# Opening, norms and the products behind them in a hybrid layer: order of the sums, engine of u's second form, banks of the transposes, order of the matmuls

## The chip, the cores and the metric

The kernel runs on one core of a Trainium2 chip. The core has TensorE (PE in the profile; its weight load is PEld), VectorE (DVE), ScalarE (ACT), GpSimd (POOL) and SyncE (SP), which issues most transfers. The metric is the device time of one execution in microseconds; the kernel before has a median of 1338.59 us over 3 runs (1337.43 to 1339.16).

## The reference

One layer over 512 tokens of 1024 channels, all in f32, with nine modulation vectors (three shifts sh, three scales sc, three gates g) made from one conditioning vector c:

```
mod = silu(c) @ w_ada + b_ada                    # 9 vectors of 1024
u = rms_norm(x, g1n) * (1 + sc1) + sh1
x = x + 0.5 * g1 * swiglu(u, ffn1_w_in, ffn1_w_out)      # hidden width 2816
u = rms_norm(x, mix_norm_g) * (1 + sc2) + sh2
z = u @ w_mix + b_mix        # q, k, v, o and gates of an mLSTM; q, k, v and gate of 16 attention heads; 2 merge gates
merged = sigmoid(g_a) * (mlstm branch @ w_branch_a) + sigmoid(g_b) * (attention branch @ w_branch_b)
x = x + g2 * (merged @ w_out)
u = rms_norm(x, ffn2_norm_g) * (1 + sc3) + sh3
x = x + 0.5 * g3 * swiglu(u, ffn2_w_in, ffn2_w_out)
```

`swiglu(u, w_in, w_out)` splits `u @ w_in` into a and b and returns `(silu(a) * b) @ w_out`. The mLSTM's q and k pass a causal convolution of width 4 first.

## The kernel before, in words

**Split products.** Every f32 product is made of three TensorE products of rounded parts: a number is split into a high part (rounded to fp32r) and a low part (the number minus its high part). `mm3` (L108 to L114) issues high × high (L112), high × low of the moving operand (L113) and low × high (L114) into one PSUM bank. `split` (L85 to L96) splits a block of weights that a transfer has put into a raw tile: ScalarE writes the high part wh (L93), VectorE the low part wl (L95). There are three raw tiles and four slots each for wh and wl, so a fifth block's split waits until the last matmul of the first block has read its slot. `w_stat` loads and splits one block of 128 output columns for all 8 channels of 128 (8 × 128 × 128 weights, a 128x1024 tile).

**u.** The normed and modulated activations are kept transposed, as eight channels k of 128 rows by 512 tokens, in two parts uh[k] and ul[k]. `xnorm` makes x times the reciprocal root of its mean square (tiles xn, L236 and L237; the sums of squares are L203, the twelve small steps of the root L129 to L139). `norm_turn` (L261) transposes xn of 256 tokens on TensorE: 16 transposes (L266) into four PSUM banks, channel k in bank k % 4, half k // 4 of the bank. Then `u_from` (L241) per channel: ScalarE reads the bank and writes uh = scale · t + shift (L245), VectorE reads the same and writes the same in full precision as uf (L249), and ul = uf − uh is made by VectorE for even k and by GpSimd for odd k (L250). `norm_half` is the norm and its transposes for one half of the tokens.

**Banks.** There are eight PSUM banks: four called g (`gbank`) for products and four called t (`tbank`), both taken in rotation. A fifth g bank is the first one again, once its reader is through.

**Who sets the order.** All code outside the opening is written in program order and laid out by the framework's planner: it builds each engine's list beforehand, from its own costs, taking the earliest in the program among what it believes ready. Each engine then works through its list strictly in order, waiting on semaphores. The opening, `start` (L680 to L901), is ordered by hand instead: each of its instructions is chained behind the one before on its engine (`queued`, L675).

**The opening.** Shift and scale of the first norm are sums over w_ada: for each block k of 128 columns, VectorE accumulates eight products of a 128x256 tile with a column of silu(c) (`product`, L777 to L786, line L784 in the trace; `ada_dve` is a run of them), TensorE adds up the 128 rows (`total`, L793), ScalarE makes the two columns m (`mods`, L797 and L798), then both uh and uf of channel k (`uh`, L803 and L804), and VectorE ul (`ul`, L806). Meanwhile TensorE multiplies the channels that are ready by the first 3 + 3 column blocks of ffn1 (`mms`, L824: 18 matmuls a channel into 6 banks), whose weights are split at L810 (`wh`) and L814 (`wl`). One round of the loop, k = 3 to 7, is: 12 matmuls of channel k − 1 with the transposes of channel k between them, `total(k)`, the first product of block k + 1 (on ScalarE), the split of the weights of k + 1, products 1 to 3 of block k + 1, `mods(k)`, `uh(k)`, `ul(k)`, products 4 to 7, and the last 6 matmuls of channel k − 1. The six banks are a0, b0, a1, b1, a2, b2 of three ffn blocks; in a channel all six get high × high first, then the product with wl, then the one with ul, except in the last channel, which goes bank by bank.

**Behind the mix norm.** ffn1's output runs in `pair_out`. Four hooks in it (`chans`) make the u's of the first 256 tokens, channels i and i + 4 at a time. Then four blocks of w_mix are multiplied with the first 256 tokens (L1318 ff.), the second half is transposed and made into u, and the same four blocks are multiplied with tokens 256 to 511, one block's bank after another (L1340). Behind that come the convolutions (`qk_conv`, L944 ff., which read those banks) and the gates' product (`gates`, L904 ff., a 128-wide stationary block of 96 columns whose weights are split at L93 from the tile rawg).

**Behind norm 3.** w_out runs over the second half of the columns, with the transposes and u's of the first 256 tokens begun before its last token block (`last`, L1455 ff.); the last three of its weight blocks stay in their slots until that token block has used them. Then `norm_half(1)`, and FFN2, which begins with `first_pair` (L568): the blocks a0, b0, a1, b1 with tokens 0 to 255, one bank after another, then the same with tokens 256 to 511; when a block's two banks are complete, `hidden` (L355) reads them: SiLU on ScalarE (L363), the product on VectorE (L364).

Of the kernel before, what the change touches and what calls it, by code (L numbers as in the profile page):

```python
# [14 lines left out]
AF = mybir.ActivationFunctionType  # L15
# [5 lines left out]
P = 128  # L21
# [27 lines left out]
class Layer:  # L49
# [190 lines left out]

    def u_from(self, ps, k, c0, w, G, sh, pool, start=False):  # L241

        nc = self.nc
        uf = self.tmp(pool, "uf")
        nc.scalar.activation(self.uh[k][:, c0:c0 + w], ps, AF.Identity, scale=G, bias=sh)  # L245
        if start:
            self.last_uf = nc.scalar.activation(uf[:, :w], ps, AF.Identity, scale=G, bias=sh)
        else:
            nc.vector.tensor_scalar(uf[:, :w], ps, G, sh, op0=MUL, op1=ADD)  # L249
        self.last_ul = (nc.gpsimd if not start and k % 2 else nc.vector).tensor_tensor(  # L250
            self.ul[k][:, c0:c0 + w], uf[:, :w], self.uh[k][:, c0:c0 + w], op=SUB)

# [8 lines left out]
    def norm_turn(self, hf, xn, G, sh, b, ks=range(NK)):  # L261

        nc = self.nc
        for k in range(NK):
            for i in range(2):
                nc.tensor.transpose(b[k % 4][:, k // 4 * 256 + i * P:k // 4 * 256 + (i + 1) * P],  # L266
                                    xn[i][k // 4][:, k % 4 * P:(k % 4 + 1) * P], self.ident)
        u = lambda k: self.u_from(b[k % 4][:, k // 4 * 256:(k // 4 + 1) * 256], k, hf * 256, 256, G[:, k:k + 1], sh[:, k:k + 1], self.tp)
        for k in ks:
            u(k)  # L270
        return u

    def gemm_stat(self, ps, w, c0, c1, ks=range(NK)):
        wh, wl = w
        for k in ks:
            self.mm3(ps[:wh.shape[2], c0:c1], wh[:, k, :], wl[:, k, :],
                     self.uh[k][:, c0:c1], self.ul[k][:, c0:c1], k == 0, k == NK - 1)


    def ada_row(self, v, accs, bank):  # L280
# [288 lines left out]
    def first_pair(self, w_in):  # L569

        js = (0, 1)
        wa = [self.w_stat(w_in, j * P) for j in js]
        wb = [self.w_stat(w_in, FF + j * P) for j in js]
        pp = [(self.gbank(), self.gbank()) for _ in js]
        for c0 in (0, 256):
            for i, j in enumerate(js):
                self.gemm_stat(pp[i][0], wa[i], c0, c0 + 256)
                self.gemm_stat(pp[i][1], wb[i], c0, c0 + 256)
                if c0:
                    self.hidden(pp[i][0], pp[i][1], j)  # L580

# [102 lines left out]
    def start(self, st, tp):  # L684
# [128 lines left out]
        def wl(k, eng=None):  # L813
# [3 lines left out]
            else:  # L817
                dve(f(V))
        order = [(b, p) for p in range(3) for b in range(2 * NJ0)]
        def mms(k, n0, n1):  # L820
            h, l = wsp[k]
            for bnk, p in (sorted(order) if k == NK - 1 else order)[n0:n1]:
                c = slice(bnk // 2 * P, (bnk // 2 + 1) * P)
# [46 lines left out]
        wh(3)  # L870
        ada_dve(3, range(0, 3))
        ul(2)
        wl(3)
        ada_dve(3, range(3, 8))
        mms(1, 12, 18)
        for k in range(3, NK):
# [5 lines left out]
            if more:  # L882
                product(k + 1, 0, AC)
                if early:
                    wh(k + 1)
                    wl(k + 1)
                ada_dve(k + 1, range(1, 4))
            mods(k)
            uh(k)
            ul(k)  # L890
            if more:
                if not early:
                    wh(k + 1)
                    wl(k + 1)
                ada_dve(k + 1, range(4, 8))
            mms(k - 1, 12, 18)
# [393 lines left out]
    def run(self):  # L1290
# [8 lines left out]
        with tc.tile_pool(name="f1t", bufs=1) as tp:  # L1299
# [4 lines left out]
            with tc.tile_pool(name="f1h", bufs=1) as fp:  # L1304
# [12 lines left out]
                def chans(i):  # L1317
                    for k in (i, i + 4):  # L1318
                        n2["u"](k)
# [18 lines left out]
        self.qk = [None] * 8  # L1338
        with tc.tile_pool(name="gates", bufs=1) as mp:
            for m in range(4):  # L1340
                self.gemm_stat(pp[m], ws[m], 256, 512)
            for m in range(4):
# [149 lines left out]
```

## Time and profile before

| | |
|---|---|
| median of 3 runs | 1338.59 us |
| the profiled execution | 1337.66 us, span 1335.9 us |
| TensorE busy | 1315.4 us, 6468 matmuls and transposes |
| VectorE / ScalarE / GpSimd busy | 938.9 / 620.7 / 162.3 us |
| read and written | 199.97 MB and 29.95 MB |
| TensorE clock | full speed in every slice |

All times are microseconds from the start of the span unless marked ns. The profiled execution's time is 1.76 us longer than the span that its trace shows. "Waits" are idle time of an engine just before an instruction, put down to the instruction that released it. A name such as `ul<-uf,uh` gives the output and the inputs of an instruction.

### The profile page before, as it was taken

The page shows a single profiled execution, that of the slowest core. Times are in us where ns is not written, and L with a number is a line of the kernel's source. Part 1 is how long each engine was busy: PE and PEld are TensorE (multiplying, and loading weights), DVE is VectorE, ACT ScalarE, POOL GpSimd, SP SyncE. Part 2 cuts the span into 40 slices and gives each one's busy share as a digit, 9 for nine tenths or more (in the row PEclk, how much of TensorE's full clock was granted, in tenths as well). Part 3 has the DMA queues.
Part 4 walks back from the last instruction along what each step waited for, and adds up shares of the span by engine and source line. Part 5 has one row for each costly group of instructions (what it writes and reads, how often), then busy time and mean ns, then how long its engine had stood idle before and what let it go on. Part 6 is the DMA issues. An engine that isn't in the chain of part 4 may idle for free.

```text
span 1335.9 us, 17955 instructions
## 1 busy us (share of the span) xinstructions
PE 1315.4 (98%) x6468; PEld 1101.6 (82%) x6468; DVE 938.9 (70%) x1706; ACT 620.7 (46%) x1056; POOL 162.3 (12%) x216
## 2 busy tenths in 40 slices
PE   7899999999999999999999999999999999999998
PEld 6688888888888888888888878888788888888887
DVE  6777687778678876876585876766676665655655
ACT  5543433326557745556565675432354333433442
POOL 2000000001020100312041311002120000000000
PEclk9999999999999999999999999999999999999999
DMA  9786576776662434444343442787527554444474
GB/s 288 226 274 204 183 235 201 258 235 225 226 161 80 135 111 124 132 116 123 79 143 87 113 128 71 231 250 229 164 88 269 189 181 159 148 151 145 154 260 142
DMA packets 228621, 231.11 MB, mean 173 GB/s; under 512 B 12274, under 2 KB 183954, under 8 KB 228532
## 3 DMA queue, kind: packets, MB, share of 16 engines
q1 hardware_dynamic: 217428, 186.34, 46.5%
q0 software_dynamic: 11040, 43.61, 8.9%
q8 instruction: 51, 0.84, 0.3%
q14 instruction: 38, 0.31, 0.1%
q10 hardware_dynamic: 64, 0.02, 0.0%
HBM read 199.97 MB, written 29.95 MB: 172 GB/s over the span
## 4 chain that ended last, share of the span: by engine, by line
PE 88%; DVE 5%; DMA 3%; ACT 2%; issue 1%; SPq 0%; POOL 0%; DVEq 0%; ACTq 0%; POOLq 0%
PE g L114 21%; PE g L113 21%; PE g L112 21%; PE t L467 2%; PE t L469 2%; PE t L468 2%; PE t L1226 2%; DMA raw<-in_ffn_w_in_dram 2%; PE t L442 1%; PE t L440 1%; PE t L441 1%; PE t L1196 1%; PE t L112 1%; PE t L113 1%; PE t L114 1%
## 5 line engine op out<-in xcount | busy, mean ns | idle before, releaser
L93 ACT ACTIVATE wh<-raw 128x1024 fp32r<-128x1024 f32 x218 | 226.6, 1043 | 385.8 <-PE g L113 99.1
L113 PE MATMUL g<-ul,wh 128*128 128x512 f32 (+2 forms) x984 | 369.9, 376 | 1.1 <-DVE ul L250 0.8
L112 PE MATMUL g<-uh,wh 128*128 128x512 f32 (+2 forms) x984 | 370.1, 377 | 0.7 <-ACT sl L363 0.7
L114 PE MATMUL g<-uh,wl 128*128 128x512 f32 (+2 forms) x984 | 369.6, 376 | 0.2 <-DVE wl L95 0.2
L95 DVE TENSOR_TENSOR wl<-raw,wh 128x1024 fp32r<-128x1024 f32 x218 | 267.2, 1229 | 143.0 <-ACT wh L93 135.9
L113 PEld LDWEIGHTS g<-ul,wh 128*128 128x128 f32 (+1 forms) x984 | 184.9, 188 | 34.7 <-DVE ul L250 1.0
L112 PEld LDWEIGHTS g<-uh,wh 128*128 128x128 f32 (+1 forms) x984 | 184.6, 188 | 34.5 <-ACT sl L363 1.1
L114 PEld LDWEIGHTS g<-uh,wl 128*128 128x128 f32 (+1 forms) x984 | 184.8, 188 | 34.0 <-DVE wl L95 0.4
L112 PE MATMUL g<-wh,uh 128*128 128x512 f32 (+1 forms) x320 | 111.9, 350 | 0.0
L114 PE MATMUL g<-wh,ul 128*128 128x512 f32 (+1 forms) x320 | 111.1, 347 | 0.0
L113 PE MATMUL g<-wl,uh 128*128 128x512 f32 (+1 forms) x320 | 111.0, 347 | 0.0
L291 DVE SCALAR_TENSOR_TENSOR acc<-raw,ccol,acc 128x1024 f32<-128x1024 f32 (+1 forms) x63 | 65.8, 1060 | 41.9 <-DMA raw<-in_w_ada_dram 41.8
L112 PEld LDWEIGHTS g<-wh,uh 128*128 128x128 f32 x320 | 60.5, 189 | 7.8 <-DVE tk L1080 0.5
L114 PEld LDWEIGHTS g<-wh,ul 128*128 128x128 f32 x320 | 60.5, 189 | 7.8
L113 PEld LDWEIGHTS g<-wl,uh 128*128 128x128 f32 x320 | 60.5, 189 | 7.4
L364 DVE TENSOR_TENSOR hp<-g,sl 128x512 f32<-128x512 f32 x43 | 29.5, 688 | 50.2 <-PE g L114 49.4
L430 POOL DMA_DIRECT2D S_d<-rw x22 | 12.2, 555 | 322.7 <-DVE rw L425 303.9
L112 PE MATMUL g<-yl,wh 128*128 128x512 f32 x128 | 50.3, 393 | 0.0
L113 PE MATMUL g<-yl,wh 128*128 128x512 f32 x128 | 50.3, 393 | 0.0
L114 PE MATMUL g<-yl,wl 128*128 128x512 f32 x128 | 50.3, 393 | 0.0
L417 ACT ACTIVATE wh<-rw 128x1024 fp32r<-128x1024 f32 x22 | 23.3, 1057 | 49.5 <-issue 35.7
L1178 ACT ACTIVATE S<-S,mn 128x128 f32<-128x128 f32 (+1 forms) x64 | 35.6, 557 | 20.1 <-DVE mn L1170 12.6
(337 smaller groups left out, 2304.2 us busy)
## 6 DMA issues: line engine op xcount, KB each, us to landing
raw<-in_ffn_w_in_dram SPq DMA_DIRECT2D x82, 512.0 KB, 3.9
raw<-in_w_ada_dram SPq DMA_DIRECT2D x56, 512.0 KB, 4.1
raw<-in_w_mix_dram SPq DMA_DIRECT2D x48, 512.0 KB, 4.1
rw<-in_ffn_w_out_dram POOLq DMA_DIRECT2D x20, 1024.0 KB, 7.1
S_d<-rw POOLq DMA_DIRECT2D x22, 768.0 KB, 4.0
raw<-S_d SPq DMA_DIRECT2D x30, 512.0 KB, 3.8
raw<-in_w_mix_dram SPq DMA_DIRECT2D x32, 256.0 KB, 3.0
ar<-in_w_ada_dram SPq DMA_DIRECT2D x14, 512.0 KB, 7.8
```

The costliest lines, as they stand in the source:

```text
L93: self.last_hi = nc.scalar.activation(hi, src, AF.Copy)
L95: self.last_lo = self.last_wl = (eng or nc.vector).tensor_tensor(lo, src, hi, op=SUB)
L112: mm(ps, lh, rh, start=start, stop=False)
L113: mm(ps, lh, rl, start=False, stop=False)
L114: self.last_mm = mm(ps, ll, rh, start=False, stop=stop)
L291: nc.vector.scalar_tensor_tensor(a, r[:, cut(i)], self.ccol[:, k:k + 1], a, op0=MUL, op1=ADD)
L364: nc.vector.tensor_tensor(h, ps_b[:, c0:c1], s[:, :c1 - c0], op=MUL)
L467: mm(ps[t], a[0], wh[:, k, :], start=first and c + k == 0, stop=False, skip_group_check=True)
L468: mm(ps[t], a[0], wl[:, k, :], start=False, stop=False, skip_group_check=True)
L469: mm(ps[t], a[1], wh[:, k, :], start=False, stop=end, skip_group_check=True)
L1178: nc.scalar.activation(S[:, ws], S[:, ws], AF.Exp, scale=-1.0, bias=m, accum_out=sm[:, qb:qb + 1])
L1226: nc.tensor.matmul(po[:, q0:], vt[pr][:, kb, i % 2, :], Px[:, o:o + T - q0], start=n == 1, stop=n == 8)
```

## The change

Four places are edited.

- `u_from`: ScalarE writes both uh and uf, and VectorE alone makes ul, for every channel.
- `norm_turn`: channel k is put into bank k // 2, half k % 2, so that two neighbouring channels share a bank; the hooks in ffn1's output make channels 2i and 2i + 1 at a time.
- A new function `gemms` multiplies channel by channel over four banks. `first_pair` uses it for all channels of the first 256 tokens, and for channels 0 to 5 of the others; channels 6 and 7 then follow per block (its two banks), with SiLU and product behind each block. The products of the mix norm's second half do the same: channels 0 to 5 over the four banks, then 6 and 7 bank by bank.
- The opening: one product of the sums more stands ahead of each `ul` (products 1 to 4 before and 5 to 7 after it, in place of 1 to 3 and 4 to 7; for block 3, products 0 to 3, `ul(2)`, products 4 to 7, then the split's low part). The last channel's 18 matmuls begin with the eight that need no ul in banks 0 to 3, then the four with ul, then banks 4 and 5.

```diff
-    def u_from(self, ps, k, c0, w, G, sh, pool, start=False):
+    def u_from(self, ps, k, c0, w, G, sh, pool):
...
         nc.scalar.activation(self.uh[k][:, c0:c0 + w], ps, AF.Identity, scale=G, bias=sh)
-        if start:
-            self.last_uf = nc.scalar.activation(uf[:, :w], ps, AF.Identity, scale=G, bias=sh)
-        else:
-            nc.vector.tensor_scalar(uf[:, :w], ps, G, sh, op0=MUL, op1=ADD)
-        self.last_ul = (nc.gpsimd if not start and k % 2 else nc.vector).tensor_tensor(
-            self.ul[k][:, c0:c0 + w], uf[:, :w], self.uh[k][:, c0:c0 + w], op=SUB)
+        nc.scalar.activation(uf[:, :w], ps, AF.Identity, scale=G, bias=sh)
+        self.last_ul = nc.vector.tensor_tensor(self.ul[k][:, c0:c0 + w], uf[:, :w], self.uh[k][:, c0:c0 + w], op=SUB)
...
-                nc.tensor.transpose(b[k % 4][:, k // 4 * 256 + i * P:k // 4 * 256 + (i + 1) * P],
+                nc.tensor.transpose(b[k // 2][:, k % 2 * 256 + i * P:k % 2 * 256 + (i + 1) * P],
...
+    def gemms(self, ps, ws, c0, c1, ks=range(NK)):
+        for k in ks:
+            for p, w in zip(ps, ws):
+                self.gemm_stat(p, w, c0, c1, (k,))
...
         for c0 in (0, 256):
-            for i, j in enumerate(js):
-                self.gemm_stat(pp[i][0], wa[i], c0, c0 + 256)
-                self.gemm_stat(pp[i][1], wb[i], c0, c0 + 256)
-                if c0:
-                    self.hidden(pp[i][0], pp[i][1], j)
+            banks, ws = [p for q in pp for p in q], [w for q in zip(wa, wb) for w in q]
+            self.gemms(banks, ws, c0, c0 + 256, range(6 if c0 else NK))
+            for i, j in enumerate(js if c0 else ()):
+                self.gemms(pp[i], (wa[i], wb[i]), 256, 512, (6, 7))
+                self.hidden(pp[i][0], pp[i][1], j)
...
+        close = sorted(order[:12], key=lambda t: t[0] > 1)
+        close = close[:4] + [(2, 0), (2, 1), (3, 0), (3, 1), (0, 2), (1, 2), (2, 2), (3, 2)] + [(b, p) for b in (4, 5) for p in range(3)]
...
-            for bnk, p in (sorted(order) if k == NK - 1 else order)[n0:n1]:
+            for bnk, p in (close if k == NK - 1 else order)[n0:n1]:
...
-        ada_dve(3, range(0, 3))
+        ada_dve(3, range(0, 4))
         ul(2)
+        ada_dve(3, range(4, 8))
         wl(3)
-        ada_dve(3, range(3, 8))
...
-                ada_dve(k + 1, range(1, 4))
+                ada_dve(k + 1, range(1, 5))
...
-                ada_dve(k + 1, range(4, 8))
+                ada_dve(k + 1, range(5, 8))
...
-                    for k in (i, i + 4):
+                    for k in (2 * i, 2 * i + 1):
...
+            self.gemms(pp, ws, 256, 512, range(6))
             for m in range(4):
-                self.gemm_stat(pp[m], ws[m], 256, 512)
+                self.gemm_stat(pp[m], ws[m], 256, 512, (6, 7))
```

More of the change, by code (lines that the diff above doesn't have):

```diff
@@ L265, in norm_turn @@
             for i in range(2):
-                nc.tensor.transpose(b[k % 4][:, k // 4 * 256 + i * P:k // 4 * 256 + (i + 1) * P],
+                nc.tensor.transpose(b[k // 2][:, k % 2 * 256 + i * P:k % 2 * 256 + (i + 1) * P],
                                     xn[i][k // 4][:, k % 4 * P:(k % 4 + 1) * P], self.ident)
-        u = lambda k: self.u_from(b[k % 4][:, k // 4 * 256:(k // 4 + 1) * 256], k, hf * 256, 256, G[:, k:k + 1], sh[:, k:k + 1], self.tp)
+        u = lambda k: self.u_from(b[k // 2][:, k % 2 * 256:(k % 2 + 1) * 256], k, hf * 256, 256, G[:, k:k + 1], sh[:, k:k + 1], self.tp)
         for k in ks:
```

## Prediction

> **What bounds the kernel now.** I read the profile's page first (its busy times and the chain that ended last), then the waits of TensorE, then windows and timelines around the places that the diff touches.
>
> ```profile
> PE 1315.4 (98%) x6468; PEld 1101.6 (82%) x6468; DVE 938.9 (70%) x1706; ACT 620.7 (46%) x1056; POOL 162.3 (12%) x216
> ...
> PE 88%; DVE 5%; DMA 3%; ACT 2%; issue 1%; SPq 0%; POOL 0%; DVEq 0%; ACTq 0%; POOLq 0%
> ```
>
> TensorE (PE) is busy for 1315.4 of the span of 1335.9 us, so it idles for 20.5 us in all, and the chain runs through it for 88%. The edits add and remove no matmul. They can shorten the time only where PE waits, and lengthen it wherever they let PE wait anew. The waits of PE that stand at lines the edits touch:
>
> ```profile
> PE t L793 <- DVE ac L784: 2.6, 3, 1.4
> PE g L824 <- ACT uh L803: 1.6, 2, 1.2
> ...
> PE g L113 <- DVE ul L250: 0.8, 1, 0.8
> PE g L112 <- ACT sl L363: 0.7, 1, 0.7
> PE g L824 <- DVE ul L806: 0.7, 1, 0.7
> ...
> PE g L113 <- POOL ul L250: 0.3, 1, 0.3
> ```
>
> (columns: total us, times, longest.) Without L112's, which no edit aims at, they sum to 6.0 us, 0.45% of the span: that is the ceiling of what can be won. L793, L803 and L806 lie in the opening, L250 behind the mix norm. None of the five lies behind norm 3, which the edits touch too.
>
> **Part A, the opening** (one more product of the modulation's sum ahead of each ul; the last channel's matmuls in another order).
>
> ```profile
> 12.00:47.40 35.40, 31.91 (x180) 25.43 (x179) 27.31 (x62) 17.91 (x33) 0.00 (x0) 1.00 1.15 307
> ...
> 47.40 0.85 ACT L810 ACTIVATE wh<-raw 128x768 fp32r<-128x768 f32 x1 [2.77 <-DMA raw<-in_ffn_w_in_dram]
> ```
>
> (Windows: bounds, length, busy time of PE, PE's weight load, VectorE, ScalarE and GpSimd, then clock, DMA share, GB/s. Timelines: start, duration, engine, line, operation, and in brackets the idle time before it and what ended that.) Until 47.40 us the transfers are the limit: their share is 1.15 at 307 GB/s, and ScalarE stands 2.77 us until the weights of channel 6 land at 47.40. ScalarE's list is in order, so the uh of channel 5 comes behind that split whatever VectorE did before. Whatever the longer runs of products save ahead of that moment (the L793 waits; the longest is 1.4) is therefore given back at 47.40. I cost the first re-ordering at 0 (were the landing not the limit, it would be −1.4 and more; 307 GB/s excludes that). After it:
>
> ```profile
> 56.06 0.69 DVE L806 TENSOR_TENSOR ul<-uf,uh 128x512 fp32r<-128x512 f32 x1 [0.52 <-ACT uf L804]
> 56.67 2.04 DVE L784 SCALAR_TENSOR_TENSOR ac<-ar,ccol,ac 128x256 f32<-128x256 f32 x4
> ...
> 58.76 0.71 PE L793 MATMUL t<-one,ac 128*128 128x128 f32 x4
> ```
>
> A fourth product (2.04/4 = 0.51) fills VectorE's hole of 0.52 ahead of ul, so the sum is ready at 58.2 instead of 58.7. But PE comes to it at 58.76 without having waited: its 18 matmuls and the transposes fill the time. So 0 again, at most 0.3.
>
> ```profile
> 61.23 0.39 PE L824 MATMUL g<-uh,wl 128*128 128x512 f32 x1
> ...
> 62.28 0.50 PE L824 MATMUL g<-ul,wh 128*128 128x512 f32 x1 [0.66 <-DVE ul L806]
> ...
> 66.00:257.00 191.00, 191.00 (x845) 157.73 (x843) 143.89 (x188) 69.88 (x90) 10.76 (x18) 1.00 0.70 224
> ```
>
> In the kernel before, the last channel goes bank by bank, and its third matmul waits for ul (61.23 + 0.24 to 62.28: some 0.8 with the restart). The new order issues eight matmuls that need no ul first, 8 × 0.23 = 1.9 us, so ul is there. What follows is 191 us in which PE never idles, so the gain stays. Two banks close later than they did (after the ninth and tenth matmul, not the third and sixth); the next block's hiding place is those 191 us. **A = −0.8**, bounds −1.1 (0.8 + 0.3) and +0.1 (SiLU of block 0 four matmuls, 0.9 us, later and uncovered).
>
> **Part B, behind the mix norm** (ScalarE makes uh and uf, VectorE alone ul, channels 2i and 2i+1 share a bank, products by channel over four banks). The first half of the tokens:
>
> ```profile
> 362.00:384.08 22.08, 22.08 (x103) 18.00 (x102) 17.70 (x26) 11.85 (x20) 5.79 (x4) 1.00 0.55 166
> ...
> L249 DVE TENSOR_SCALAR uf<-t,G,sh 128x256 f32<-128x256 f32 x16 | 8.0, 537 | 3.0 <-ACT uh L245 3.0
> ...
> L245 ACT ACTIVATE uh<-t,sh,G 128x256 fp32r<-128x256 f32 x16 | 7.5, 572 | 0.6 <-PE t L266 0.6
> ```
>
> (The last two are groups from norm 3, with two halves of eight: busy us, mean ns, idle time before.) Here PE is full with ffn1's output. Per half, VectorE loses 8 uf (4.0 us) and gets four more ul; ScalarE gains 8 operations at 7.5/16 = 0.47, 3.8 us on top of 11.85 in 22.08. Both fit: 0; with that cover gone the last channel's uf, 0.5, would come late. The second half is where PE waits:
>
> ```profile
> 395.58 1.91 PE L266 MATMUL t<-ident,xn 128*128 128x128 f32 x16
> ...
> 396.88 3.77 ACT L245 ACTIVATE uh<-t,sh,G 128x256 fp32r<-128x256 f32 x8 [2.28 <-PE t L266]
> ...
> 397.49 0.74 PE L112 MATMUL g<-uh,wh 128*128 128x256 f32 x4
> ...
> 399.06 0.39 PE L113 MATMUL g<-ul,wh 128*128 128x256 f32 x1 [0.83 <-DVE ul L250]
> ...
> 399.98 0.39 PE L113 MATMUL g<-ul,wh 128*128 128x256 f32 x1 [0.30 <-POOL ul L250]
> ...
> 410.74 0.39 PE L112 MATMUL g<-uh,wh 128*96 128x512 f32 x1
> ```
>
> 96 matmuls stand between 397.49 and the gates' first at 410.74: 13.25 us for 96 × 0.121 = 11.6, so 1.6 are lost. In the new order bank 0 is full after four transposes instead of ten, so uh starts 6 × 0.12 = 0.7 earlier, at 396.2; then 2 × 0.47 = 0.94 a channel on ScalarE against 12 × 0.121 = 1.45 on PE. The ul of channel 0 is out at 397.8, when PE has done the four matmuls that it can without it. No stall is left: −1.6. Against it, the slot and bank of the first weights, which are used through to the last channels:
>
> ```profile
> 404.58 0.84 ACT L93 ACTIVATE wh<-rawg 128x768 fp32r<-128x768 f32 x1 [3.94 <-PE g L113]
> ...
> 405.46 0.96 DVE L95 TENSOR_TENSOR wl<-rawg,wh 128x768 fp32r<-128x768 f32 x1 [1.85 <-ACT wh L93]
> ```
>
> The split of the gates' weights waits for the slot of the first block, freed at 404.6. Now that is 78 matmuls after 397.4, 406.8; wh and wl are through at 406.8 + 0.84 + 0.96 = 408.6, with PE due at 409.1. It holds by 0.5. If ScalarE or VectorE takes a conv operation first, one turn for a 1024-wide weight (1.06 + 1.22, rows below) lies bare: −1.6 + 2.3 = +0.7. **B = −1.6**, bounds −1.7 and +1.2 (that, and the 0.5 of the first half). I take the low end, because the planner put this split ahead of the conv before.
>
> **Part C, behind norm 3.** Nothing waits there, but the weights stand in ScalarE's list behind the u's:
>
> ```profile
> 978.99 3.74 ACT L245 ACTIVATE uh<-t,sh,G 128x256 fp32r<-128x256 f32 x8
> 982.59 2.99 ACT L93 ACTIVATE wh<-raw 128x1024 fp32r<-128x1024 f32 x3
> 987.05 0.63 ACT L203 ACTIVATE rs<-x 128x512 f32<-128x512 f32 x1 [1.48 <-DVE x L670]
> ...
> 985.14 1.22 DVE L95 TENSOR_TENSOR wl<-raw,wh 128x1024 fp32r<-128x1024 f32 x1
> ...
> 986.41 0.39 PE L114 MATMUL g<-uh,wl 128*128 128x256 f32 x1 [0.15 <-DVE wl L95]
> ...
> 982.12:1008.15 26.03, 25.74 (x209) 24.99 (x208) 17.88 (x40) 14.08 (x22) 6.37 (x8) 1.00 0.55 175
> ...
> 1008.15:1100.00 91.85, 91.85 (x408) 76.04 (x407) 58.78 (x81) 33.12 (x44) 5.04 (x8) 1.00 0.61 201
> ```
>
> PE starts ffn2's first pair at 982.12 with one weight block split (a0); the other three are split at 982.59, behind eight uh, and PE waits for the first of them already (986.41). The first pair takes 26.03 us for 192 × 0.12 + 1.8 of transposes = 24.85: 1.2 of loss. Now sixteen operations stand ahead: 978.99 + 16 × 0.47 = 986.5. With the L203 that comes in (0.6) the first wh ends at 988.1 and its wl (1.22) at about 989.2. Until then PE has a0 alone, 24 matmuls, and some four of the other banks that take a wh whose wl is still missing: 28 × 0.12 = 3.4 of 7.1 us, 3.7 idle, where 1.2 were: **+2.5**, and products by channel over four banks make it no shorter, since three of the four banks have no weights. If the splits slip in between the u's it is 0.
>
> VectorE's uf would have cost 537 ns where ScalarE's costs 572: as single operations they are equal, and what I charge is the queue. [...]
>
> At the end of the pair:
>
> ```profile
> 1000.00 1.06 ACT L93 ACTIVATE wh<-raw 128x1024 fp32r<-128x1024 f32 x1 [3.08 <-issue]
> 1001.08 1.28 ACT L363 ACT_TABLE_LOAD   x1
> 1002.37 0.60 ACT L363 ACTIVATE sl<-g 128x512 f32<-128x512 f32 x1
> ```
>
> Block 2 needs a0's weight slot and a0's bank, read by SiLU (sl). Both were free by 1003.0, five us ahead of 1008.15. With channels 6 and 7 left to the end, a0 closes some 15 matmuls, 1.8 us, before the pair ends. Then wh 1.06, table load 1.28 and sl 0.60 follow in ScalarE's order: −1.8 + 2.9 + 0.2 of handing over = **+1.3**. Bounds 0 (another order) and 2.4 (one more split of 1.06 ahead of sl). **C = +3.8**, bounds 0 and +4.9. I take the value near the upper end, since the rows show the u's ahead of the splits. After 1008.15 PE is full for 92 us, so nothing is given back.
>
> **Sum:** −0.8 − 1.6 + 3.8 = +1.4 us. The profiled execution took 1337.66 (1.76 around its span), so 1339.1; the median of the runs shown, 1338.59, lies 0.93 above the profiled one, which gives 1340.0.
>
> **The rivals.**
> *Weights in time.* The planner sets ScalarE's order by what it believes ready, and could take the splits between the sixteen u's, or close the pair early. Then C = 0, and −2.4 is left: 1336.2. For it: 982.59 follows the u's without a gap, so the trace doesn't tell when the splits became possible. Against: they come later in the program than the u's, and the last of w_out's blocks holds their slots until 982.
>
> *Late release, the slower side.* Products by channel over four banks end all four blocks within some 5 us, so weight slots and banks come free late at both places. Behind the mix norm one turn of 2.3 us lies bare, behind norm 3 2.4: −0.8 + 0.7 + 4.9 = +4.8, 1343.4. It decides once the gates' wl is ready later than 409.1, against 408.6 worked out above. For it: 0.5 us of slack, with the conv's operations on the same two engines. Against: before, the split went first.
>
> *It doesn't do what it says.* The opening's waits are the transfers' and the stall behind the mix norm only moves to the gates, while norm 3 hides its u's: 0, 1338.6.
>
> **How the numbers follow.** A measurement of this kernel tells 0.2%, 2.7 us, from no change: faster is below 1335.9, slower above 1341.3. The forecast has 0.50 (its own range 1338.0 to 1341.4), weights in time 0.24, late release 0.18, no effect 0.08. Faster: 0.17 from the second, 0.02 from the first, 0.19. Slower: 0.16 from the third, 0.10 from the first, 0.26. Same: 0.55. The bounds sum to −2.8 and +6.2. Behind each place the planner lays its order anew; the wait of L112 for SiLU, 0.7, is one that could go or come with it, which makes −3.5, 1335.1, and +6.9, 1345.5. The range, 1335.3 to 1344.0, leaves out only where nearly all bounds meet.
>
> **What would show it.** Step A: L824's wait for ul gone, the other L793 waits shorter but 47.40 unmoved. B: no wait of L113 on ul, gates' first matmul 1.6 us sooner behind the transposes. C: PE idle for 3 to 4 us around 987 to 989, waiting for wl L95, and 1.3 before block 2, waiting for sl. The forecast is wrong if the splits of norm 3 stand between the u's, or if the gates wait for wl.

## The result, and the profile after

The changed kernel is slower: a median of 1342.05 us over 12 runs (1340.15 to 1343.26) against 1337.66 us over 12 runs of the kernel before (1336.70 to 1339.16). The ratio is 1.0031, with a 95% interval of 1.0023 to 1.0038. The profiled execution took 1342.87 us with a span of 1341.1, so it is one of the longer ones; its trace holds 5.2 us more than the trace before.

From the page of the profile, the busy times and the chain that ended last, and then the waits of TensorE (total us, times, longest) in the changed kernel:

```profile
PE 1318.9 (98%) x6468; PEld 1104.5 (82%) x6468; DVE 929.9 (69%) x1690; ACT 632.3 (47%) x1087; POOL 145.6 (11%) x200
...
PE 86%; DVE 6%; ACT 4%; DMA 3%; issue 2%; SPq 0%; ACTq 0%; DVEq 0%
```

```profile
PE g L827 <- ACT uh L804: 3.5, 2, 2.3
PE g L112 <- ACT sl L364: 1.3, 2, 1.1
PE g L113 <- DVE ul L247: 1.2, 4, 0.3
PE g L112 <- ACT wh L93: 0.9, 1, 0.9
...
PE t L943 <- issue: 0.8, 1, 0.8
...
PE t L794 <- DVE ac L785: 0.3, 1, 0.3
```

The same 6468 matmuls and transposes keep TensorE busy 3.5 us longer than before: from 50.20 to 53.61 us and from 988.86 to 992.28 the clock is 0.50. Of the waits that the edits aimed at, those for VectorE's sums (L794, 2.6 before) and for the last ul of the opening are all but gone. In their place stand a longer wait for uh in the opening, and behind norm 3 waits for ul, wh and SiLU that weren't there before.

TensorE works through its list in order, so the k-th matmul of one trace can be set against the k-th of another. The table gives how much earlier (−) or later the matmul at each landmark of the trace before comes in the profiled execution of every kernel (kernels and labels below), and how long FFN2's first pair takes from its first matmul to the next block's:

| kernel | 66.1 us: first product behind the opening | 395.6: transposes of the mix norm's second half | 410.7: gates | 469.9 | 982.1: first pair begins | first pair |
|---|---|---|---|---|---|---|
| before | 0 | 0 | 0 | 0 | 0 | 26.03 |
| changed | −0.28 | +0.30 | −1.19 | +0.04 | +0.16 | 30.93 |
| open_only | −1.47 | −1.48 | −1.46 | −1.46 | −1.42 | 26.02 |
| sums_old | −1.14 | −0.70 | −2.20 | −0.94 | −0.94 | 30.94 |
| fill | −1.29 | −1.41 | −2.91 | −2.07 | −2.14 | 30.89 |
| mix_only | −0.03 | −0.12 | −1.63 | −0.36 | −0.21 | 26.02 |
| n3_old | +0.17 | −0.36 | −1.86 | −0.73 | −0.73 | 26.02 |
| mix_close | −1.09 | −0.75 | −2.25 | −1.01 | −1.00 | 26.02 |
| n3_u_vector | −1.32 | −1.08 | −2.58 | −1.37 | −1.44 | 28.25 |
| n3_by_block | −0.52 | −0.05 | −1.55 | −0.29 | −0.23 | 30.00 |
| n3_half | −0.24 | +0.31 | −1.19 | +0.02 | +0.01 | 27.10 |
| n3_hi_vector | +0.07 | +2.48 | +0.98 | +1.82 | +1.80 | 26.56 |
| best | −0.80 | +1.83 | +0.33 | +0.33 | +0.32 | 26.03 |
| final | −0.25 | +0.74 | −0.75 | −0.73 | −0.66 | 25.66 |

In the changed kernel's trace the opening brings 0.3, which is lost again by 120 us (+0.3); the mix norm brings 1.5 at 411 us and has lost 1.2 of it by 470; the first pair of FFN2 costs 4.9. After 1020 us nothing moves any more.

A part of the column at 66.1 us is not the edits' doing. The weights of channel 6 land at another moment in each execution (46.92 us in fill, 47.40 before, 48.16 in final), and wherever TensorE waits for the uh behind them, its next matmul starts 2.10 us after the landing, before and after the change (49.50 before, 49.30 in the changed kernel, 50.26 in final, behind landings at 47.40, 47.20 and 48.16). With the landings set equal, the column reads −0.08 to −0.11 for changed, n3_old, n3_by_block, n3_half and n3_hi_vector, −1.13 and −1.11 for open_only and n3_u_vector, −0.94, −0.99 and −1.01 for sums_old, mix_close and final, and −0.81 and −0.78 for fill and best.

**The opening.** Its timelines on ScalarE and TensorE, and the two stretches around 50 us (columns as in the prediction; in the windows the clock is the third number from the end):

```profile
47.20 0.84 ACT L811 ACTIVATE wh<-raw 128x768 fp32r<-128x768 f32 x1 [3.77 <-DMA raw<-in_ffn_w_in_dram]
```

```profile
46.37 0.62 PE L827 MATMUL t<-ul,wh 128*128 128x512 f32 x2
49.30 1.37 PE L827 MATMUL g<-uh,wh 128*128 128x512 f32 x4 [2.31 <-ACT uh L804]
```

```profile
46.79:50.20 3.41, 1.10 (x5) 0.75 (x5) 2.05 (x4) 2.96 (x6) 0.00 (x0) 1.00 0.46 119
50.20:53.61 3.41, 3.41 (x12) 2.72 (x11) 3.30 (x7) 0.85 (x2) 0.00 (x0) 0.50 0.55 157
...
982.28:985.45 3.17, 2.61 (x19) 2.19 (x18) 1.39 (x4) 3.17 (x9) 0.00 (x0) 1.00 0.00 0
985.45:988.86 3.41, 1.89 (x11) 1.28 (x11) 3.25 (x6) 3.41 (x8) 0.00 (x0) 1.00 0.13 49
988.86:992.28 3.42, 3.42 (x18) 3.42 (x17) 3.21 (x10) 1.08 (x3) 0.00 (x0) 0.50 0.70 202
982.28:1013.21 30.93, 27.71 (x209) 26.48 (x207) 13.90 (x34) 19.40 (x37) 0.74 (x1) 0.94 0.47 161
```

The weights of channel 6 land at 47.20 as they did before (47.40), and TensorE, which now reaches that point 2 us earlier, stands there for 2.31 us in one piece. In the kernel before, the wait at this place was 0.43 us:

```profile
49.50 1.19 PE L824 MATMUL g<-uh,wh 128*128 128x512 f32 x4 [0.43 <-ACT uh L803]
```

In the changed kernel's 3.41 us to 50.20 it is busy for 1.10; in the next 3.41 us its clock is 0.50, and four 128x512 matmuls take 1.90 us at 52.03, where four take 1.17 at 54.59. The rows behind that show the same at norm 3: 1.89 of 3.41 busy, then 3.42 us at 0.50, in which 128x256 matmuls start 0.21 us apart, against 0.12 from 992.54 on.

**The mix norm.**

```profile
397.54 0.36 PE L112 MATMUL g<-uh,wh 128*128 128x256 f32 x1
398.05 0.39 PE L113 MATMUL g<-ul,wh 128*128 128x256 f32 x1
...
409.55 0.39 PE L112 MATMUL g<-uh,wh 128*96 128x512 f32 x1
...
433.33 0.43 PE L943 MATMUL t<-ident,ggm 64*128 64x64 f32 x4 [0.78 <-issue]
```

```profile
432.61 0.63 ACT L933 ACTIVATE ggm<-gfs 4x512 f32<-4x512 f32 x1
```

No stall of L113 is left, and the gates start 1.5 us sooner behind the transposes. But the gates' four small transposes now stand 18 matmuls earlier in TensorE's list than before, where they ran without a wait:

```profile
437.73 0.46 PE L940 MATMUL t<-ident,ggm 64*128 64x64 f32 x4
```

In the changed kernel TensorE reaches them at about 432.4, and ggm isn't written before 433.24: 0.78 us of waiting, though the row names no releaser. With the restart that is 0.85 of the 1.2 that are lost; the other 0.35 go at 438.86, where a weight load of TensorE waits for wl:

```profile
438.86 0.19 PEld L113 LDWEIGHTS g<-wl,uh 128*128 128x128 f32 x1 [0.53 <-DVE wl L95]
```

**Norm 3 and FFN2's first pair.**

```profile
985.84 0.65 ACT L246 ACTIVATE uf<-t,sh,G 128x256 f32<-128x256 f32 x1
986.29 2.09 ACT L93 ACTIVATE wh<-raw 128x1024 fp32r<-128x1024 f32 x2
...
1010.20 1.06 ACT L93 ACTIVATE wh<-raw 128x1024 fp32r<-128x1024 f32 x1 [7.12 <-PE g L113]
1011.27 1.28 ACT L364 ACT_TABLE_LOAD   x1
1012.57 1.09 ACT L364 ACTIVATE sl<-g 128x512 f32<-128x512 f32 x2
```

```profile
984.27 0.38 PE L113 MATMUL g<-ul,wh 128*128 128x256 f32 x1 [0.27 <-DVE ul L247]
...
988.44 0.39 PE L112 MATMUL g<-uh,wh 128*128 128x256 f32 x1 [0.91 <-ACT wh L93]
...
1013.21 0.50 PE L112 MATMUL g<-uh,wh 128*128 128x512 f32 x1 [1.14 <-ACT sl L364]
```

The splits begin behind the sixteenth u operation, at 986.29 instead of 982.59. TensorE, which has only a0's weights until then, first waits for four ul (1.2 us in all), then for wh (0.9). At the end the split of block 2, the table load and SiLU follow one another on ScalarE, and TensorE waits for SiLU.

### The profile page after: what moved, and what is told of

Its sections match the earlier page's. It is cut to its first block, busy times and chain, and to the rows that moved or that the text cites. A ratio compares the mean times of both kernels' runs of the same rounds, so it can differ in the third digit from the quotient of the medians.

```text
span 1341.1 us, 17944 instructions
## 1 busy us (share of the span) xinstructions
PE 1318.9 (98%) x6468; PEld 1104.5 (82%) x6468; DVE 929.9 (69%) x1690; ACT 632.3 (47%) x1087; POOL 145.6 (11%) x200
## 4 chain that ended last, share of the span: by engine, by line
PE 86%; DVE 6%; ACT 4%; DMA 3%; issue 2%; SPq 0%; ACTq 0%; DVEq 0%
PE g L113 20%; PE g L112 20%; PE g L114 20%; PE t L468 2%; PE t L470 2%; PE t L469 2%; PE t L1229 2%; PE t L443 1%; PE t L442 1%; PE t L441 1%; DMA raw<-in_ffn_w_in_dram 1%; DVE wl L95 1%; PE g L827 1%; PE t L1199 1%; PE t L112 1%
## 5 line engine op out<-in xcount | busy, mean ns | idle before, releaser
L113 PE MATMUL g<-ul,wh 128*128 128x512 f32 (+2 forms) x984 | 371.3, 377 | 1.3 <-DVE ul L247 1.2
L113 PEld LDWEIGHTS g<-ul,wh 128*128 128x128 f32 (+1 forms) x984 | 185.8, 189 | 35.4 <-DVE ul L247 2.3
L113 PE MATMUL g<-wl,uh 128*128 128x512 f32 (+1 forms) x320 | 111.1, 347 | 0.1
L113 PEld LDWEIGHTS g<-wl,uh 128*128 128x128 f32 x320 | 60.5, 189 | 7.9 <-DVE wl L95 0.5
L113 PE MATMUL g<-yl,wh 128*128 128x512 f32 x128 | 50.3, 393 | 0.0
```

Source lines behind the costliest of these rows:

```text
L113: mm(ps, lh, rl, start=False, stop=False)
```

## Experiments

All ratios are to runs of the kernel before on the same chip, with the 95% interval; differences of a median under some 1 us are not resolved by these runs, so the table above carries the smaller ones, each from one execution. The diffs are shortened; remarks behind a # stand for lines left out.

### Norm 3: queue, order or both

**n3_old** undoes everything at norm 3:

```diff
-    # norm 3: uf on ScalarE, ul on VectorE, channel k in bank k // 2, first_pair by channel over four banks
+    # norm 3: uf on VectorE, odd ul on GpSimd, channel k in bank k % 4, first_pair one bank after another
```

> The changed kernel with norm 3 and FFN2's first pair as before (u's second form on VectorE, odd low parts on GpSimd, old banks, one bank after another); the opening and the mix norm stay changed. All theories: the first pair takes 26.0 us again instead of 30.9, no half-speed stretch near 989, and the time is 5 us below the changed kernel, about 1337, that is at or just below the kernel before (ratio 0.9990 to 1.0003).

Measured: 1337.42 us, ratio 0.9995 (0.9985 to 1.0004); the pair takes 26.02 us. So the slowing lies here: it is 4.9 us in the trace, and without it the change is neither faster nor slower by what can be measured.

**n3_u_vector** puts back the engines alone:

```diff
-        nc.scalar.activation(uf[:, :w], ps, AF.Identity, scale=G, bias=sh)
-        self.last_ul = nc.vector.tensor_tensor(...)
+        nc.vector.tensor_scalar(uf[:, :w], ps, G, sh, op0=MUL, op1=ADD)        # at norm 3
+        self.last_ul = (nc.gpsimd if k % 2 else nc.vector).tensor_tensor(...)
```

> The changed kernel with only the engines of norm 3's u's as before; the products by channel over four banks stay. Theory of the queue (sixteen operations of ScalarE stand ahead of the weights' splits, TensorE starves, and a half-speed stretch of 3.4 us follows): the splits start at 982 to 983 again, the wait for wh and the half-speed stretch go, the wait of 1.1 us for SiLU at the pair's end stays; the pair takes 27.2 to 27.6 us, the time is about 3.5 us below the changed kernel, 1338.5. Rival, the order of the products itself: the pair stays near 30 us.

Measured: 1339.18 us, 1.0008 (0.9999 to 1.0017); the pair takes 28.25 us. TensorE's waits from 975 to 1015 us:

```profile
PE g L112 <- ACT sl L370: 1.2, 1, 1.2
PE t L268 <- DVE xn L236: 0.6, 1, 0.6
PE g L112 <- ACT wh L93: 0.2, 1, 0.2
```

The wait for wh shrinks from 0.9 to 0.2 and no stretch runs at half clock (the mean clock of this execution is 1.000). The splits start even sooner than expected, before the pair begins at 980.68 and between the u's:

```profile
979.74 1.07 ACT L93 ACTIVATE wh<-raw 128x1024 fp32r<-128x1024 f32 x1
```

But the pair is longer than the expected 27.2 to 27.6, and 2.2 us of the 4.9 stay with the order of the products: the wait for SiLU, as expected, and waits of 0.8 more in front of it.

**n3_by_block** puts back the order alone, with ScalarE making all u's:

```diff
-            self.gemms(banks, ws, c0, c0 + 256, range(6 if c0 else NK))
-            for i, j in enumerate(js if c0 else ()):
-                self.gemms(pp[i], (wa[i], wb[i]), 256, 512, (6, 7))
-                self.hidden(pp[i][0], pp[i][1], j)
+            for i, j in enumerate(js):
+                self.gemm_stat(pp[i][0], wa[i], c0, c0 + 256)
+                self.gemm_stat(pp[i][1], wb[i], c0, c0 + 256)
+                if c0:
+                    self.hidden(pp[i][0], pp[i][1], j)
```

> The changed kernel with only FFN2's first pair in the old order, one bank after another; ScalarE still makes all sixteen u forms. Theory of the queue: the wait for wh at about 988 stays and with it the half-speed stretch in most executions, the wait for SiLU at the end goes; the pair takes 29.3 to 29.9 us, the time about 1.3 us below the changed kernel, 1340.7. Rival, the order of the products itself: the pair goes back to 26 us and the time to 1337.

Measured: 1341.57 us, 1.0025 (1.0016 to 1.0034); the pair takes 30.00 us. TensorE's waits from 975 to 1015 us:

```profile
PE g L113 <- DVE ul L247: 1.1, 4, 0.3
PE g L112 <- ACT wh L93: 0.9, 1, 0.9
```

The wait for SiLU is gone, the others stay, and so does the half-speed stretch (clock 0.50 from 988.73 to 992.14). The rival, by which the order alone costs everything, falls. The two causes are 4.0 and 2.2 us alone and 4.9 together. I take it that they share the idle time at the start, where three of the four banks lack weights; no run shows this by itself. The transposes' new banks stand in n3_u_vector, n3_by_block and n3_half alike, so what they cost or save at norm 3 isn't told apart.

**n3_half** is n3_u_vector with the second 256 tokens block by block:

```diff
-            self.gemms(banks, ws, c0, c0 + 256, range(6 if c0 else NK))
+            if not c0:
+                self.gemms(banks, ws, 0, 256)
             for i, j in enumerate(js if c0 else ()):
-                self.gemms(pp[i], (wa[i], wb[i]), 256, 512, (6, 7))
+                self.gemm_stat(pp[i][0], wa[i], 256, 512)
+                self.gemm_stat(pp[i][1], wb[i], 256, 512)
```

> As n3_u_vector (norm 3's u's on the engines of before, changed opening and mix norm), with the first pair's products by channel only for the first 256 tokens; the second 256 run one bank after another as before. Theory of the late release (SiLU reads a0's bank only 1.8 us ahead of the pair's end): the wait for sl of 1.2 goes, the pair takes 26.6 to 27.0 us instead of 28.2; time 1.4 below n3_u_vector, 1337.8. Rival, the loss sits in the first half: the pair stays at 27.8 or above.

Measured: 1338.63 us, 1.0003 (0.9994 to 1.0012); the pair takes 27.10 us, and no wait for SiLU is left. So the late release at the end is worth 28.25 − 27.10 = 1.15 us. The other 1.1 lies ahead of that, and the pair is somewhat above the 26.6 to 27.0 expected.

**n3_hi_vector** is the changed kernel with the splits moved out of ScalarE's list:

```diff
-        wa = [self.w_stat(w_in, j * P) for j in js]
-        wb = [self.w_stat(w_in, FF + j * P) for j in js]
+        wa = [self.w_stat(w_in, j * P, hi_v=j > 0) for j in js]      # hi_v: VectorE makes wh
+        wb = [self.w_stat(w_in, FF + j * P, hi_v=True) for j in js]
```

> The changed kernel with one edit: the high parts of the first pair's last three weight blocks are made on VectorE, so that they don't stand behind the sixteen u operations in ScalarE's list. Theory of the queue: no wait for wh near 988, no half-speed stretch there, the wait for sl at the end stays; the pair takes 27.3 to 28.5 us instead of 30.9, time 2.5 to 3.5 below the changed kernel, 1339. Rival, the pace of the u's themselves (0.9 us a channel on ScalarE) holds TensorE: the pair stays at 30 us or above.

Measured: 1337.91 us, 0.9999 (0.9990 to 1.0009); the pair takes 26.56 us, less than was expected. The first copy on VectorE, and all that TensorE waits for from 975 to 1015 us:

```profile
981.33 0.69 DVE L90 CAST wh<-raw 128x1024 fp32r<-128x1024 f32 x1 [1.26 <-PE g L114]
```

```profile
PE g L112 <- ACT sl L364: 1.1, 1, 1.1
```

This settles the queue: with ScalarE still making sixteen forms at the same pace, the waits for ul and wh and the half-speed stretch are gone as soon as the splits don't stand behind them: 128x256 matmuls start 0.12 us apart from 983.92 to 987.95. The row also shows when the first slot comes free: TensorE's matmul releases it at 981.3, well ahead of the sixteenth u operation (987.49 in this trace). VectorE's copy takes 0.69 us where ScalarE's takes 1.06.

### The opening and the clock

**open_only** is the kernel before with the two edits of the opening:

```diff
-                ada_dve(k + 1, range(1, 4))      # and 4 to 7 behind ul; block 3: 0 to 2, ul, wl, 3 to 7
+                ada_dve(k + 1, range(1, 5))      # and 5 to 7 behind ul; block 3: 0 to 3, ul, 4 to 7, wl
-            for bnk, p in (sorted(order) if k == NK - 1 else order)[n0:n1]:
+            for bnk, p in (close if k == NK - 1 else order)[n0:n1]:
```

> The kernel before with only the two edits of the opening. Prediction's step A: TensorE's waits ahead of 47 us shrink and are given back at the landing of 47.4, the last channel's stall goes, so FFN1's products come 0.8 us earlier than before and the time is 0.8 lower, 1336.9. Theory of the window: the waits are gathered into one gap of 2.3 us, a half-speed stretch follows in most executions and takes back 0.5 to 1; gain at 66 us 0 to 0.3, time 1337.4 to 1337.9, and lower in executions without the stretch.

Measured: 1338.20 us, 1.0000 (0.9991 to 1.0009), and −1.47 us at 66 us in its trace. Its gap is nearly that of the changed kernel, and no half-speed stretch follows in this execution (four 128x512 matmuls take 1.20 us at 49.16 and 1.18 at 51.01):

```profile
46.37 0.62 PE L826 MATMUL t<-ul,wh 128*128 128x512 f32 x2
49.16 1.20 PE L826 MATMUL g<-uh,wh 128*128 128x512 f32 x4 [2.18 <-ACT uh L803]
```

The same opening thus gives −1.47 and −1.32 (n3_u_vector) without such a stretch, and −0.52 to +0.17 (changed, n3_old, n3_by_block, n3_half, n3_hi_vector) with it; the mean clocks of these executions are 0.999 and 1.000 without it, 0.996 to 0.999 with it. With the landings set equal these are −1.1 and −0.1, so the stretch costs about 1.0 us. The median shows no gain, and open_only's eleven times fall in two groups: four of 1336.02 to 1336.62, the profiled one among them, and seven of 1338.04 to 1339.56, of which no trace is kept. What holds these seven up is not shown.

**sums_old** is the changed kernel with the sums in their old runs and the last channel's new order:

```diff
-                ada_dve(k + 1, range(1, 5))      # and 5 to 7 behind ul; block 3: 0 to 3, ul, 4 to 7, wl
+                ada_dve(k + 1, range(1, 4))      # and 4 to 7 behind ul; block 3: 0 to 2, ul, wl, 3 to 7
```

> The changed kernel with the sums of the opening in their old runs (one product fewer ahead of each ul) and the last channel's new order kept. Theory of the window: TensorE's idle time ahead of 49.5 is spread over three gaps again, none over 1.4 us, no half-speed stretch at 50; FFN1's products come 0.5 to 0.8 us earlier than in the changed kernel, time 1341.3. Rival (the longer runs did gain): they come later by 0.3 to 0.5.

Measured: 1341.78 us, 1.0029 (1.0018 to 1.0040), which doesn't differ from the changed kernel by what the medians tell. In the traces it is at −1.14 at 66 us, 0.86 earlier than the changed kernel, with no half-speed stretch in the opening (mean clock 0.998 against 0.997); mix_close, with the same opening, is at −1.09. With the landings set equal both are near −1.0, and so is final: the last channel's order is worth 1.0. The longer runs then add 0.1 to 0.2 where no stretch follows, and lose about 0.9 where one does.

**fill** puts transposes of a constant into the gap:

```diff
             mms(k - 1, 12, 18)
+            if k == 5:
+                for i in range(16):
+                    pe(lambda: PE.transpose(cb[:, 128:256], self.ident, self.ident))
```

> The changed kernel with 16 transposes of a constant, unused, put into TensorE's gap ahead of the matmuls of channel 5 in the opening (46.99 to 49.30 us). Theory of the window (a gap of 2.3 us inside one stretch of 3.4 us makes the next 3.4 us run at half clock): no half-speed stretch between 50 and 54 us, the matmuls of channel 5 still start at 49.3, and all that follows comes 1.0 to 1.5 us earlier; time about 1 us below the changed kernel, 1341. Rival, the half clock there has another cause: it stays, and the time doesn't move or rises by up to 0.3.

Measured: 1341.01 us, 1.0023 (1.0014 to 1.0032). The stretch is gone and 66 us is reached at −1.29, 1.0 ahead of the changed kernel (0.7 with the landings set equal). But the filling didn't run as I meant:

```profile
48.21 1.97 PE L902 MATMUL t<-ident 128*128 128x128 f32 x16 [1.47 <-ACT m L799]
49.93 1.18 PE L827 MATMUL g<-uh,wh 128*128 128x512 f32 x4
```

The transposes write the bank that ScalarE reads for m, waited for that, and pushed the real matmuls to 49.93, though the weights landed at 46.92 here. They split the gap rather than filling it: 1.47 us of waiting stay ahead of them, and behind them four matmuls take 1.18 us, as in the kernel before (1.19 at 49.50). In the trace of best below the same transposes stand behind 1.48 us of waiting, and four matmuls take 1.18 us at 50.39. But open_only has 2.18 us of waiting in one piece, and four matmuls in 1.20 us behind it. That the half clock follows from the gap agrees with the changed kernel, fill and best; it is not shown.

### The mix norm, and what beats both

**mix_only** is the kernel before with the mix norm's edits (the diff is the change's without the opening, `norm_half` and `first_pair`):

```diff
-                    for k in (i, i + 4):
+                    for k in (2 * i, 2 * i + 1):
...
+            self.gemms(pp, ws, 256, 512, range(6))
             for m in range(4):
-                self.gemm_stat(pp[m], ws[m], 256, 512)
+                self.gemm_stat(pp[m], ws[m], 256, 512, (6, 7))
```

> The kernel before with only the mix norm's edits (ScalarE's second form, pairs of channels in a bank, products by channel over four banks). Prediction's step B: the gates' products begin 1.5 us earlier behind the transposes and that stays: time 1336.1. Theory that it is given back: of the 1.5 us some 1.2 are lost again by 456 us, where TensorE meets the gates' small transposes too early or the weights of the next blocks late; time 1337.3.

Measured: 1337.64 us, 1.0000 (0.9991 to 1.0009). The 1.5 us are there at 411 us and 1.3 of them are lost by 470. The waits of TensorE from 405 to 475 us hold a single row, where the kernel before has none:

```profile
PE t L948 <- issue: 0.8, 1, 0.8
```

**mix_close** is mix_only with the last channel's order:

```diff
-            for bnk, p in (sorted(order) if k == NK - 1 else order)[n0:n1]:
+            for bnk, p in (close if k == NK - 1 else order)[n0:n1]:
```

> The changed kernel with the old runs of sums in the opening and norm 3 as before: the last channel's new order and the mix norm's edits are what is left. If both gains stay: 0.8 and 0.3 to 1.5 below the kernel before, 1335.4 to 1336.6, ratio 0.9984 to 0.9993. If they are lost to what follows: 1337.4 or above, ratio 0.9998.

Measured: 1336.08 us, 0.9987 (0.9978 to 0.9996): faster than the kernel before.

**best** chains the gates' transposes behind a later product, with the opening of fill and the old norm 3:

```diff
-                if m == 6:
+                if m == 7:
                     with tc.issue_after(self.last_mm.ins):
                         columns()
```

> The opening as changed, with the 16 unused transposes in TensorE's gap; the mix norm as changed, with the gates' four small transposes chained behind the seventh instead of the sixth block's products; norm 3 and FFN2's first pair as before. If the opening's gain stays without the half-speed stretch (1.3) and the loss between 411 and 470 us is the wait of those transposes for ggm (0.8 and its restart): 66 us is reached 1.3 earlier, the 1.5 of the mix norm loses 0.4 at most, 2.4 in all at the end; time 1335.3, ratio 0.9978 to 0.9986. Rival, the loss there is VectorE's and ScalarE's later chain as such: 1.2 of the 1.5 are lost as before, time 1336.5.

Measured: 1335.90 us, 0.9988 (0.9979 to 0.9996). The opening brings 0.80, not the 1.3 expected. From 411 to 470 us nothing is lost (+0.33 at both), and no wait of TensorE is left between 405 and 475 us. So what took back the mix norm's gain was those four transposes' place in the order. The profiled execution is a late one for another reason: it loses 2.6 us between 300 and 380, at a wait for SiLU of 1.8 us with a half-speed stretch behind it (128x512 matmuls start 0.43 us apart from 302.04 to 304.60, 0.23 until 299.19). The wait stands at the same place in the kernel before, with 0.7.

**final** puts together what gained, as a diff to the changed kernel those of sums_old, best (`m == 7` alone), n3_hi_vector and n3_half's order. ScalarE makes the u's at norm 3.

> The parts that the runs so far show to gain: the last channel's new order with the old runs of sums (1.0 to 1.1 earlier at 66 us); the mix norm as changed, with the gates' small transposes chained behind the seventh block's products (1.5 earlier at 411 us, kept at 470); norm 3's u's on ScalarE with the high parts of the first pair's last three weight blocks on VectorE, products by channel for the first 256 tokens and one bank after another for the second. If they add up: the pair takes 25.2 to 25.8 us (26.6 with VectorE's splits, less the wait of 1.1 for sl), 2.8 to 3.3 in all, time 1334.8, ratio 0.9975 to 0.9984. Rival, the pair loses at its start what it gains at its end (26.5 or more): ratio 0.9982 to 0.9990.

Measured: 1335.64 us against 1338.62, 0.9976 (0.9967 to 0.9985). The pair takes 25.66 us, within what was expected and below the 26.03 of the kernel before. In the profiled execution the opening is only 0.25 early, since the weights of channel 6 landed 0.8 later than before:

```profile
48.16 0.85 ACT L813 ACTIVATE wh<-raw 128x768 fp32r<-128x768 f32 x1 [3.27 <-DMA raw<-in_ffn_w_in_dram]
```

This version beats both kernels.

## Why the prediction was right and wrong

The time, 1342.05, lies within the range (1335.3 to 1344.0) but past the own range of the forecast (1338.0 to 1341.4). I had put 0.55 on no change and 0.26 on slower; it is slower. The sum was +1.4, and the traces show +5.2, the medians +4.4. Everything that the sum had wrong lay on the same side.

- **A, the opening: −0.8 forecast, −0.3 measured**, of which 0.2 is the landing's. The last channel's order is worth 1.0, where I had 0.8 with a bound of 1.1. The step that failed is "I cost the first re-ordering at 0". Its reasoning held: the landing (47.20) decided, and the earlier savings were given back there. But they were given back as one gap of 2.3 us, and TensorE's next 3.4 us ran at half clock, which cost about 1.0. I counted a gathered wait as equal to the same wait in pieces.
- **What followed the opening.** "What follows is 191 us in which PE never idles, so the gain stays" was wrong in that trace by 0.6: at 97.7 TensorE waited 0.27 for hp, queued on VectorE behind a product whose weights had landed late (96.26, against 94.53 before). VectorE's timeline in the changed kernel:

```profile
96.26 0.75 DVE L294 TENSOR_SCALAR acc<-raw,ccol 128x1024 f32<-128x1024 f32 x1 [7.62 <-DMA raw<-in_w_ada_dram]
96.93 0.68 DVE L365 TENSOR_TENSOR hp<-g,sl 128x512 f32<-128x512 f32 x1
```

  From 66 to 120 us the traces lose between nothing (n3_u_vector, with the same opening) and 0.6, so this varies with the execution.
- **B, behind the mix norm: −1.6 forecast.** The step itself measured −1.5 in every kernel that has it, and the gates' split came in time (PE due at 409.1 worked out, 409.55 in the trace, in which the transposes start 0.3 late). The late-release rival isn't what happened here. What failed is that I left the sum there: the planner set the gates' transposes 18 matmuls, some 4 us, earlier in TensorE's list, and 1.2 of the 1.5 went. Among the bounds I had allowed 0.7 for the planner's new order, without naming this place.
- **C, behind norm 3: +3.8 forecast, +4.9 measured.** The mechanism was right in both halves: the splits stood behind the sixteen u's, and SiLU came late at the end. The splits started at 986.3 (986.5 worked out); a0 was alone until then; sl held TensorE at the end for 1.14 (1.3 worked out, 1.15 by n3_half). The term that was mis-sized is the idle time at the start, +2.5: alone it measured +4.0 in n3_by_block, since a stretch at half clock follows it. That stretch gets through 3.42 × 0.50 = 1.7 us less work, which I didn't have; the 2.3 that remain are near the 2.5. The waits themselves were not those that I named: none for wl, but 1.2 us for four ul, since ScalarE's two forms of a channel take 0.9 us and TensorE's three matmuls 0.36, and 0.9 for wh. That +4.9 is also my upper bound for C is luck, since the bound had one more split ahead of sl, which didn't come. That "products by channel over four banks make it no shorter" is too mild: in n3_half they cost 1.1 in the first half (together with the new banks) even with the u's made as before.
- **ScalarE's pace.** ScalarE's sixteen operations ran from 978.47 to 986.29, with one L203 of 0.62 between: 0.45 each, under the 0.47 of the row that I took. With uf on VectorE the pair was shorter, 28.25 us (n3_u_vector) against 30.93, but by way of the queue: n3_hi_vector keeps the u's on ScalarE and takes 26.56.
- **The rivals.** Weights in time (0.24) did not happen in the changed kernel; n3_hi_vector, which has the weights sooner by another way, shows that it would have been worth about 4.4. Late release (0.18) named the right place at norm 3 (sl) but priced it at 2.4, where 1.1 was measured, and its turn of 2.3 behind the mix norm didn't come. That its total, +4.8, is nearer to the result than the forecast's is luck. That nothing would change (0.08) had norm 3 hide its u's, and it didn't.

## What to carry to other kernels

An engine's operation that is moved to another engine is to be priced by what stands behind it in that engine's list, here three weight splits, and not by its own duration. A wait that is only gathered in one place isn't always neutral: behind the 2.31 us of the changed kernel 3.41 us ran at half clock, behind the 0.93 us that final, with the old runs of sums, has there none did, and with the landings set equal 0.9 us lies between them; so several short waits can be cheaper than a long one, though behind open_only's 2.18 us the clock stayed full. A landing that TensorE waits for shifts all that follows, so it is to be taken off before two traces are compared. A gain under a planner that lays the whole order anew is only safe when followed past the next few instructions that it may move; chaining four transposes to a later product kept 1.2 us here.

## What the runs showed of the hardware

TensorE's clock is 0.50 from 50.20 to 53.61 us and from 988.86 to 992.28 in the changed kernel's trace, and from 988.73 to 992.14 in n3_by_block's: 3.41 or 3.42 us each. Idle time stands ahead of each of them: TensorE is busy for 1.10 of the 3.41 us to 50.20, for 1.89 of the 3.41 us to 988.86 and, in n3_by_block, for 2.22 of the 3.73 us to 988.73; in best, 1.82 us of waiting end at 301.40, shortly ahead of its slow matmuls. But 2.18 us of waiting were followed by full speed in open_only, and 0.7 us in the kernel before where best has its 1.82. What length or place of the idle time decides it, these runs don't show. The profile page's row of the clock doesn't show such stretches: it has a 9, which is 90% or more, in all 40 slices of both kernels, though the clock is at half for 3.41 us twice in the changed one, and at the end of both (0.53 from 1340.40 us in the changed kernel, 0.51 from 1333.30 before).

The stretches at half clock fit most of the spread of the changed kernel. One such stretch lowers an execution's mean clock by 3.41 × 0.5 / 1341 = 0.0013. Of the 12 runs two have a mean clock of 0.999 (1340.15 and 1340.17 us), six 0.998 (1340.53 to 1342.59, mean 1341.53), four 0.997 (1342.82 to 1343.26, mean 1343.04): about 1.4 us from one to the next. It is not exact, because the half-speed stretch at the kernel's very end, 0.7 us in the changed kernel's trace and 2.6 in the one before, lowers the mean too. In open_only it doesn't fit: its executions at a mean clock of 1.000 run from 1336.02 to 1339.56 us.

Open remains why the wait for SiLU near 301 us runs from 0.2 us (changed) to 1.8 (best) between executions whose code is the same there, which moved single traces by up to 2.6 us, and why the gap of 2.31 us was followed by half clock in the changed kernel and that of 2.18 us in open_only wasn't.
